# A two-block transformer step on one core: sums of squares as float32r products of a high and a low part

## The chip, the core and the metric

The kernel runs on one core of a Trainium2 chip. The metric is device microseconds of one execution, lower is better. Names: TensorE (PE; PEld is its weight load) does matrix products, VectorE (DVE) and ScalarE (ACT) elementwise work, GpSimd (POOL) little here, SyncE (SP) starts the DMAs.

## The reference, cut to what matters

One input of 256 rows of 1024 features (16 extra rows ahead in the first half) passes through two blocks. Everything is float32. The norms are what the change touches:

```
def rms_norm(x, g):                     # over all 1024 features, and over 64 of a head
    ms = mean(x * x, axis=-1)
    return x * rsqrt(ms + EPS) * g

# first block
h = h + 0.5 * swiglu(rms_norm(h), ...)                      # "f1", "d1"
# token mixer on rms_norm(h): two attentions of 8 heads
qa, ka = rms_norm(heads of h @ w_in)                        # each head of 64 by itself
qb, kb = rms_norm(heads of h @ w_in)
y = sigmoid(ga) * (attention(qa, ka, va) @ w) + sigmoid(gb) * (attention(qb, kb, vb) @ w)
h = h + y @ w_out
h = h + 0.5 * swiglu(rms_norm(h), ...)                      # "f2", "d2"
# second block: convolution and retention, cross attention, MLP, each on rms_norm(h)
```

So there are six norms over rows on the way (first FFN, token mixer, second FFN, second mixer, cross attention, MLP), a last one at the output that the change leaves alone, and head norms for 4 tiles of keys and 4 of queries of the first attention, 1 tile of keys and 4 of queries of the second: 13.

## The kernel before

Features lie on partitions (8 tiles of 128), rows of the sequence on the free axis (272 columns with the extra rows, else 256). Every large product is taken as three float32r products (`mm3`, lines 512 to 514): weight high x activation high, high x low, low x high. The weights come from memory in chunks of up to 2048 columns; `W.piece` cuts a piece of 1024 columns in two: ScalarE copies it rounded (`hi`, line 321), VectorE subtracts (`lo`, line 337). Three buffers each hold `raw`, `hi` and `lo`, so a new `hi` waits until TensorE has done with the chunk three back.

The order is written out by hand. `step` (a unit: 24 products or more on TensorE) first splits what the unit needs, issues the unit's products (`mm`), then a `hook` behind the split of the weights to come, and then the evacuations of the unit before, generators that give way to a weight piece at each `yield` and move to the next unit at `yield LATER`. What is issued stands in its engine's queue in that order.

The sums of squares over partitions are products with a constant matrix. `rms` (line 558), called as the hook of the first unit of a stage, multiplies `ones` (1/1024 everywhere) with `acc`, the squares summed over the 8 tiles, in float32, and takes the inverse root on ScalarE (lines 555, 556); every evacuation of the stage needs its result `r`. `head_norm` (line 761) squares x on ScalarE (`sqh`, line 765) and multiplies with `bd` (1/64 within a head), in float32 (line 767); the root follows a unit later. `key_like` and `query_like` call it in the unit after the projection. Between them on VectorE stand x (lines 803, 814), the writes of keys (line 828, six for a tile) and queries (lines 837, 851), and the values' multiplies (line 859), whose transposes (lines 865 to 867) stand on TensorE. The scores' first pass of the softmax is line 673, the transposes of its result lines 690 to 692.

PSUM has 8 banks in turn; during the two attentions three hold the results and five go round.

Of the kernel before, what the change touches and what calls it, by code (L numbers as in the profile page):

```python
# [11 lines left out]
F32R = mybir.dt.float32r  # L12
I32 = mybir.dt.int32
AF = mybir.ActivationFunctionType
# [3 lines left out]
P = 128  # L18
D = 1024
KD = D // P  # L20
SEQ = 256
NMETA = 16
T1 = SEQ + NMETA
# [341 lines left out]
LATER = object()  # L365
# [64 lines left out]
def _program(ctx, tc, I, out, probe=None):  # L430
    nc = tc.nc
    V, S, T = nc.vector, nc.scalar, nc.tensor
    probe = probe or (lambda name, ap: None)
    ctx.enter_context(tc.manual_schedule())
    base = ctx.enter_context(tc.tile_pool(name="base", bufs=1))
# [7 lines left out]
    def name(s):  # L443
        uid[0] += 1
        return f"{s}_{uid[0]}"
# [3 lines left out]
    def bank():  # L449

        turn[0] = (turn[0] + 1) % 8
        if spare[0] and turn[0] >= 5:
            return bank_o()
        return psum.tile([P, 512], F32, tag="ps", bufs=5, name=name("ps"))

    def bank_o():
        return psum_o.tile([P, 512], F32, tag="po", bufs=3, name=name("po"))

    def tmp(pool, tag, n=TP, bufs=2, dt=F32):
        t = pool.tile([P, -(-n // LINE) * LINE if pool is base else n], dt, tag=tag, bufs=bufs, name=name(tag))  # L460
        return t[:, :n]
# [3 lines left out]
    use, step, background = core.use, core.step, core.background  # L465
# [26 lines left out]
    def k0(n):  # L492
        o, w = _CST0[n]
        return c0[:, o : o + w]

    def kc(n):
        o, w = _CST[n]
        return cst[:, o : o + w]

    def c2(ap):  # L500
        return ap.rearrange("p (s c) -> p s c", c=P)
# [14 lines left out]
    def high(h_, src, gain=None):  # L516
        if gain is None:
            S.activation(h_, src, AF.Copy)
        else:
            S.activation(h_, src, AF.Copy, scale=gain)  # L520

    def low(l_, src, h_, gain=None):
        if gain is None:
            V.tensor_tensor(l_, src, h_.bitcast(F32), op=ALU.subtract)
        else:
            V.scalar_tensor_tensor(l_, src, gain, h_.bitcast(F32), op0=ALU.mult, op1=ALU.subtract)  # L526
# [25 lines left out]
    def rsqrt(dst, src):  # L552

        use(LN_EXP)
        S.activation(dst, src, AF.Ln, bias=k0("eps")[: dst.shape[0]])
        S.activation(dst, dst, AF.Exp, scale=-0.5)

    def rms(acc, n):

        ps = bank()  # L560
        T.matmul(ps[:, :n], k0("ones"), acc, start=True, stop=True)
        r = tmp(base, "r")
        rsqrt(r[:, :n], ps[:, :n])
        return r

    def xs(k, n=SEQ):
        return XH[:, k, :n], XL[:, k, :n]

    def next_acc():
        return tmp(base, "acc")  # L570
# [21 lines left out]
    def ffn(f, d, n, h, gain, acc_in, acc_out, bg, together):  # L592
        with tc.tile_pool(name="ffn" + f, bufs=2, reuse_waits="tile") as pool:
# [5 lines left out]
            def stats():  # L599
                r.append(rms(acc_in[:, :n], n))  # L600
# [127 lines left out]
    def mixer(acc_in, acc_out):  # L728
        with tc.tile_pool(name="mixer", bufs=1, reuse_waits="tile") as pool:
# [28 lines left out]
            def project(tag, ms, evac, n=SEQ, width=P, **kw):  # L758
                products(tag, ms, lambda k: xs(k, n), evac, late=1, out=lambda t: t[:width, :n], **kw)

            def head_norm(x, n):


                sq = tmp(pool, "sqh")[:, :n]
                S.activation(sq, x, AF.Square)
                ss = bank()
                T.matmul(ss[:, :n], kc("bd"), sq, start=True, stop=True)

                def root():
                    rc = tmp(pool, "rc")[:, :n]  # L770
                    rsqrt(rc, ss[:, :n])
                    return rc

                return root
# [26 lines left out]
            def key_like(ps, write):  # L801
                x = tmp(pool, "x", bufs=4)[:, :T1]
                V.tensor_tensor(x, ps[:, :T1], r[0][:, :T1], op=ALU.mult)
                yield
                root = head_norm(x, T1)
                yield LATER
                rc = root()
                yield
                for e in range(2):
                    write(e, slice(64 * e, 64 * e + 64), x, rc)  # L810

            def factor(dst, ps, turned):
                order = backwards if turned else lambda ap: ap
                V.tensor_tensor(dst, order(c2(ps[:, :SEQ])), order(c2(r[0][:, :SEQ])), op=ALU.mult)

            def query_like(ps, write, turned=False):
                x = tmp(pool, "x", bufs=4)[:, :SEQ]
                factor(c2(x), ps, turned)
                root = head_norm(x, SEQ)
                yield LATER  # L820
                rc = root()
                yield
                write(x, rc)
# [63 lines left out]

            use(LN_EXP)
            project("ka", (0, 1, 2), key, T1, hook=lambda: r.append(rms(acc_in[:, :T1], T1)))
            project("ka", (3,), key, T1)  # L890
            for m in range(4):
# [652 lines left out]
    acc = next_acc()  # L1544
# [6 lines left out]
    for k in range(KD):  # L1551
        squares(acc[:, :T1], hA[:, k, :T1], k, T1)()
        if k % 4 == 3:
            W.piece(2 * CH)
    W.split(2 * CH)
    background.append(lambda: None)
    background.append(lambda: None)
    background.append(lambda: nc.sync.dma_start(cst, I["cst"]))

    acc2 = next_acc()  # L1560
    with tc.tile_pool(name="early", bufs=1, side="right") as early:
# [8 lines left out]
    acc, acc2 = acc2, next_acc()  # L1570
# [3 lines left out]
    acc, acc2 = acc2, next_acc()  # L1574
# [11 lines left out]
    acc, acc2 = acc2, next_acc()  # L1586
    with tc.tile_pool(name="kvm", bufs=1, side="right", reuse_waits="tile") as kv:
# [5 lines left out]
        acc, acc2 = acc2, next_acc()  # L1593
        cross(acc, acc2, kx, vx, rm, held)
        probe("h5", hB)
    acc, acc2 = acc2, next_acc()
# [17 lines left out]
```

## Time and profile before

| | |
|---|---|
| median of three runs | 960.11 us (959.51 to 960.20) |
| the profiled execution | 959.74 us, its span 958.0 us |
| TensorE busy | 939.4 us, 98% |
| VectorE busy | 672.9 us, 70% |
| ScalarE busy | 534.7 us, 56% |
| HBM read | 166.79 MB, 175 GB/s over the span |

A busy share is taken over the whole span. Matmul records overlap, since they are pipelined: their distance from start to start tells what one costs in a stream. The profiled execution lies 0.37 us under the median of the three runs.

### The profile page before, as it was taken

To read this page: it belongs to the slowest core of one execution; us is meant where nothing else is said; L and a number is where in the kernel's file an instruction comes from. 1 tells how busy PE (TensorE), PEld (TensorE's weight loads), DVE (VectorE), ACT (ScalarE), POOL (GpSimd) and SP (SyncE) were. 2 spreads that over 40 slices of the span, in tenths; PEclk is the share of its full clock that TensorE was granted. 3 is DMA by queue.
4 is the path that set the end of the run, shared out by engine and by line. 5 is a ranking of instruction groups with operands and counts; after the bars stand their busy time and mean duration, and the time that the engine had idled before them with its cause. 6 is when DMAs were issued, how large, how long until landed. Compare 5 with 4: busy or idle time off the path is not lost.

```text
span 958.0 us, 18402 instructions
## 1 busy us (share of the span) xinstructions
PE 939.4 (98%) x7667; PEld 911.9 (95%) x7667; DVE 672.9 (70%) x1249; ACT 534.7 (56%) x927; POOL 9.9 (1%) x15
## 2 busy tenths in 40 slices
PE   7999999999999999999999999999999999999996
PEld 7999999998998999999999999889899999999996
DVE  5686556667885768677666657999977577775552
ACT  7545435456585656666554447646485466554441
POOL 0000000020000000000000000000000000000000
PEclk9999999999999999999999999999999999999998
DMA  8675526544432335565545665433544256555431
GB/s 309 192 259 181 180 94 222 175 175 160 171 126 96 133 114 217 221 220 184 210 152 180 214 214 235 168 140 134 195 162 171 88 177 221 199 200 218 176 133 44
DMA packets 31364, 169.06 MB, mean 176 GB/s; under 512 B 5144, under 2 KB 8864, under 8 KB 14640
## 3 DMA queue, kind: packets, MB, share of 16 engines
q1 hardware_dynamic: 30928, 167.34, 50.1%
q8 instruction: 60, 0.98, 0.4%
q10 hardware_dynamic: 288, 0.52, 0.1%
q14 instruction: 24, 0.20, 0.1%
q0 software_dynamic: 64, 0.01, 0.0%
HBM read 166.79 MB, written 1.07 MB: 175 GB/s over the span
## 4 chain that ended last, share of the span: by engine, by line
PE 72%; ACT 1%; DVE 1%; issue 0%; DVEq 0%
PE ps L512 14%; PE ps L513 14%; PE ps L514 14%; PE po L513 7%; PE po L514 7%; PE po L512 7%; PE ps L1015 1%; PE ps L1013 1%; PE ps L1014 1%; PE ps L661 1%; PE ps L1316 1%; PE po L705 0%; PE ps L1182 0%; PE po L1354 0%; PE po L720 0%; PE ps L1354 0%
## 5 line engine op out<-in xcount | busy, mean ns | idle before, releaser
L337 DVE TENSOR_TENSOR lo<-raw,hi 128x1024 fp32r<-128x1024 f32 (+2 forms) x334 | 373.7, 1131 | 46.2 <-ACT hi L321 44.2
L321 ACT ACTIVATE hi<-raw 128x1024 fp32r<-128x1024 f32 (+2 forms) x334 | 322.3, 981 | 127.4 <-issue 40.8
L512 PE MATMUL ps<-XH,hi 128*128 128x256 f32 (+2 forms) x976 | 280.2, 287 | 6.9 <-ACT hi L321 4.4
L514 PE MATMUL ps<-XH,lo 128*128 128x256 f32 (+2 forms) x976 | 274.7, 281 | 0.8 <-DVE lo L337 0.8
L513 PE MATMUL ps<-XL,hi 128*128 128x256 f32 (+2 forms) x976 | 274.9, 282 | 0.0
L512 PEld LDWEIGHTS ps<-XH,hi 128*128 128x128 f32 (+1 forms) x976 | 183.9, 188 | 10.5 <-ACT hi L321 4.4
L513 PEld LDWEIGHTS ps<-XL,hi 128*128 128x128 f32 (+1 forms) x976 | 184.3, 189 | 1.3 <-DVE XL L526 0.5
L514 PEld LDWEIGHTS ps<-XH,lo 128*128 128x128 f32 (+1 forms) x976 | 183.9, 188 | 1.4 <-DVE lo L337 1.0
L512 PE MATMUL po<-XH,hi 128*128 128x256 f32 (+1 forms) x456 | 128.9, 283 | 0.2 <-DVE br L1079 0.2
L514 PE MATMUL po<-XH,lo 128*128 128x256 f32 (+1 forms) x456 | 127.7, 280 | 0.6 <-DVE lo L337 0.6
L513 PE MATMUL po<-XL,hi 128*128 128x256 f32 (+1 forms) x456 | 127.5, 280 | 0.0
L514 PEld LDWEIGHTS po<-XH,lo 128*128 128x128 f32 x456 | 85.7, 188 | 0.8 <-DVE lo L337 0.8
L512 PEld LDWEIGHTS po<-XH,hi 128*128 128x128 f32 x456 | 85.7, 188 | 0.6 <-DVE br L1079 0.4
L513 PEld LDWEIGHTS po<-XL,hi 128*128 128x128 f32 x456 | 85.7, 188 | 0.1
L620 ACT ACTIVATE s<-gr 128x272 f32<-128x272 f32 (+1 forms) x44 | 18.7, 426 | 104.4 <-DVE gr L618 104.4
L512 PE MATMUL ps<-AHf,hi 128*128 128x272 f32 (+1 forms) x220 | 61.9, 281 | 0.0
L513 PE MATMUL ps<-ALf,hi 128*128 128x272 f32 (+1 forms) x220 | 61.9, 281 | 0.0
L514 PE MATMUL ps<-AHf,lo 128*128 128x272 f32 (+1 forms) x220 | 61.9, 281 | 0.0
L1053 DVE SCALAR_TENSOR_TENSOR cv<-U,par,cv 128x256 f32<-128x256 f32 x120 | 50.0, 474 | 0.2 <-ACT cv L1086 0.2
L514 PE MATMUL ps<-AHm,lo 128*128 128x256 f32 x160 | 44.2, 276 | 0.0
L512 PE MATMUL ps<-AHm,hi 128*128 128x256 f32 x160 | 44.2, 276 | 0.0
L513 PE MATMUL ps<-ALm,hi 128*128 128x256 f32 x160 | 44.2, 276 | 0.0
(384 smaller groups left out, 1769.2 us busy)
## 6 DMA issues: line engine op xcount, KB each, us to landing
raw<-in_ws_dram SPq DMA_DIRECT2D x128, 1024.0 KB, 4.8
raw<-in_ws_dram SPq DMA_DIRECT2D x32, 704.0 KB, 4.2
raw<-in_ws_dram SPq DMA_DIRECT2D x3, 512.0 KB, 5.3
dec<-in_dec_dram SPq DMA_DIRECT2D x1, 1536.0 KB, 6.6
BM<-drow SPq DMA_DIRECT2D x2, 512.0 KB, 5.5
memraw<-in_mt_dram SPq DMA_DIRECT2D x1, 1024.0 KB, 6.9
hA<-in_xt_dram SPq DMA_DIRECT2D x3, 273.0 KB, 5.4
raw<-in_ws_dram SPq DMA_DIRECT2D x3, 256.0 KB, 6.0
```

Source lines behind the costliest of these rows:

```text
L321: self.nc.scalar.activation(self.hi[c][:, a:b], self.raw[c][:, a:b], AF.Copy)
L337: self.nc.vector.tensor_tensor(self.lo[c][:, a:b], self.raw[c][:, a:b], self.hi[c][:, a:b].bitcast(F32), op=ALU.subtract)
L512: T.matmul(o, w[0], x[0], start=start, stop=False)
L513: T.matmul(o, w[0], x[1], start=False, stop=False)
L514: T.matmul(o, w[1], x[0], start=False, stop=stop)
L620: S.activation(s, gr, AF.Silu)
L661: T.matmul(ps[h][:, at : at + n], lhs, rhs, start=True, stop=True)
L1013: T.matmul(ps[i], xh[:, t], wh, start=k == 0, stop=False)
L1014: T.matmul(ps[i], xl[:, t], wh, start=False, stop=False)
L1015: T.matmul(ps[i], xh[:, t], wl, start=False, stop=k == KD - 1)
L1053: V.scalar_tensor_tensor(cv[:, m], U[:, m, j : j + SEQ], prm("cw", m * 31 + j), cv[:, m], op0=ALU.mult, op1=ALU.add)
L1316: T.matmul(ps[:, qt * SEQ : (qt + 1) * SEQ], qx[:, 2 * h + j, qt * P : (qt + 1) * P], kx[:, 2 * h + j], start=j == 0, stop=j == 1)
```

## The change

A sum over partitions now takes its operand in two float32r parts: `high` copies it rounded on ScalarE, `low` subtracts on VectorE, and `sum_over` issues two float32r products with a rounded copy of the constant matrix (`wr`, made once by `exact`). The 1/1024 and 1/64 are powers of two, so the rounded matrix is the same matrix. For the heads, the square takes a buffer under the tag "rc" (two buffers), which the roots use as well; the parts have the tags "sh" and "sl" (two buffers each). In `query_like` the parts are made where the sum was, and the sum is issued behind a further `yield LATER`, one unit later. In `key_like` the sum stays in its unit. Five entries more stand in the list of background work.

```
+    def two_parts(h_, l_, x):
+        high(h_, x)
+        low(l_, x, h_)
+        return h_, l_
+
+    def sum_over(o, w, parts):
+        for i, part in enumerate(parts):
+            T.matmul(o, w, part, start=i == 0, stop=i == 1)
+
     def rms(acc, n):
+        parts = two_parts(*(tmp(base, "sq", dt=F32R)[:, :n] for i in range(2)), acc)
         ps = bank()
-        T.matmul(ps[:, :n], k0("ones"), acc, start=True, stop=True)
+        sum_over(ps[:, :n], wr[:, 0], parts)
...
+    wr = base.tile([P, 2, P], F32R, name="wr")
+    def exact(i, w):
+        high(wr[:, i], w)
...
-            def head_norm(x, n):
-                sq = tmp(pool, "sqh")[:, :n]
+            def squared_parts(x, n):
+                sq = tmp(pool, "rc", T1)[:, :n]
                 S.activation(sq, x, AF.Square)
+                return two_parts(*(tmp(pool, "s" + c, T1, dt=F32R)[:, :n] for c in "hl"), sq)
+
+            def head_norm(parts, n):
                 ss = bank()
-                T.matmul(ss[:, :n], kc("bd"), sq, start=True, stop=True)
+                sum_over(ss[:, :n], wr[:, 1], parts)
                 def root():
-                    rc = tmp(pool, "rc")[:, :n]
+                    rc = tmp(pool, "rc", T1)[:, :n]
...
             def key_like(ps, write):
-                root = head_norm(x, T1)
+                root = head_norm(squared_parts(x, T1), T1)
                 yield LATER
...
             def query_like(ps, write, turned=False):
-                root = head_norm(x, SEQ)
+                parts = squared_parts(x, SEQ)
+                yield LATER
+                root = head_norm(parts, SEQ)
                 yield LATER
...
+    exact(0, k0("ones"))
...
+    background.extend([lambda: None] * 4)
+    background.append(lambda: exact(1, kc("bd")))
```

What stands where. First ScalarE at the start of the token mixer, from the norm over rows to the fourth key; `hi` are weight pieces, `r` the root of the norm, `sqh` (then `rc`) the squares of the keys. Before:

```order
L321 ACTIVATE hi_2440<-raw_2398 128x1024 x2
L321 ACTIVATE hi_2520<-raw_2444 128x1024
L555 ACTIVATE r_2528<-ps_2526,c_72 128x272
L556 ACTIVATE r_2528<-r_2528 128x272
L321 ACTIVATE hi_2520<-raw_2444 128x1024
L765 ACTIVATE sqh_2560<-x_2556 128x272
L765 ACTIVATE sqh_2566<-x_2564 128x272
L765 ACTIVATE sqh_2572<-x_2570 128x272
L321 ACTIVATE hi_2603<-raw_2524 128x1024
L765 ACTIVATE sqh_2609<-x_2601 128x272
```

The same place after:

```order
L321 ACTIVATE hi_2448<-raw_2406 128x1024 x2
L321 ACTIVATE hi_2528<-raw_2452 128x1024
L518 ACTIVATE sq_2534<-acc_171 128x272
L555 ACTIVATE r_2541<-ps_2538,c_72 128x272
L556 ACTIVATE r_2541<-r_2541 128x272
L321 ACTIVATE hi_2528<-raw_2452 128x1024
L779 ACTIVATE rc_2573<-x_2569 128x272
L518 ACTIVATE sh_2575<-rc_2573 128x272
L779 ACTIVATE rc_2584<-x_2582 128x272
L518 ACTIVATE sh_2586<-rc_2584 128x272
L779 ACTIVATE rc_2595<-x_2593 128x272
L518 ACTIVATE sh_2597<-rc_2595 128x272
```

The norm's copy (`sq<-acc`) stands behind the weight piece ahead of the root, and each key's copy (`sh`) behind its square. The other five norms have the copy at the same place.

VectorE there, from the norm to the fourth key. Before:

```order
L337 TENSOR_TENSOR lo_2441<-raw_2398,hi_2440 128x1024 x2
L803 TENSOR_TENSOR x_2556<-ps_2435,r_2528 128x272
L337 TENSOR_TENSOR lo_2521<-raw_2444,hi_2520 128x1024
L803 TENSOR_TENSOR x_2564<-ps_2436,r_2528 128x272
L803 TENSOR_TENSOR x_2570<-ps_2437,r_2528 128x272
L803 TENSOR_TENSOR x_2601<-ps_2531,r_2528 128x272
L337 TENSOR_TENSOR lo_2521<-raw_2444,hi_2520 128x1024
```

After:

```order
L337 TENSOR_TENSOR lo_2449<-raw_2406,hi_2448 128x1024 x2
L524 TENSOR_TENSOR sq_2535<-acc_171,sq_2534 128x272
L822 TENSOR_TENSOR x_2569<-ps_2443,r_2541 128x272
L337 TENSOR_TENSOR lo_2529<-raw_2452,hi_2528 128x1024
L524 TENSOR_TENSOR sl_2576<-rc_2573,sh_2575 128x272
L822 TENSOR_TENSOR x_2582<-ps_2444,r_2541 128x272
L524 TENSOR_TENSOR sl_2587<-rc_2584,sh_2586 128x272
L822 TENSOR_TENSOR x_2593<-ps_2445,r_2541 128x272
L524 TENSOR_TENSOR sl_2598<-rc_2595,sh_2597 128x272
L822 TENSOR_TENSOR x_2629<-ps_2544,r_2541 128x272
L337 TENSOR_TENSOR lo_2529<-raw_2452,hi_2528 128x1024
L524 TENSOR_TENSOR sl_2640<-rc_2637,sh_2639 128x272
```

Ahead of the first key stands the norm's subtraction (`sq<-acc,sq`), and between one key's multiply and the next the subtraction `sl`.

VectorE again, from the fourth query's multiply to that of the first value unit (`x` and `rep`). Before:

```order
L814 TENSOR_TENSOR x_2793<-po_2726,r_2528 128x256
L337 TENSOR_TENSOR lo_2761<-raw_2720,hi_2760 128x1024
L837 SCALAR_TENSOR_TENSOR qz<-x_2751,gq,rc_2799 64x256 x2
L778 TENSOR_TENSOR p_2831<-ps_2768,r_2528 8x272
L779 TENSOR_SCALAR p_2831<-p_2831,par 8x272
L780 SCALAR_TENSOR_TENSOR p_2832<-p_2831 8x272
L837 SCALAR_TENSOR_TENSOR qz<-x_2793,gq,rc_2839 64x256 x2
L859 TENSOR_TENSOR x_2869<-ps_2806,r_2528 128x256
L861 TENSOR_TENSOR rep_2871<-ps_2806,r_2528 128x128
```

After:

```order
L833 TENSOR_TENSOR x_2833<-po_2761,r_2541 128x256
L524 TENSOR_TENSOR sl_2838<-rc_2835,sh_2837 128x256
L337 TENSOR_TENSOR lo_2801<-raw_2757,hi_2800 128x1024
L858 SCALAR_TENSOR_TENSOR qz<-x_2742,gq,rc_2844 64x256 x2
L797 TENSOR_TENSOR p_2876<-po_2808,r_2541 8x272
L798 TENSOR_SCALAR p_2876<-p_2876,par 8x272
L799 SCALAR_TENSOR_TENSOR p_2877<-p_2876 8x272
L858 SCALAR_TENSOR_TENSOR qz<-x_2786,gq,rc_2887 64x256 x2
L880 TENSOR_TENSOR x_2917<-ps_2851,r_2541 128x256
L882 TENSOR_TENSOR rep_2919<-ps_2851,r_2541 128x128
```

The last query's pair of multiplies (`qz`) no longer stands ahead of the value unit's `x`, the third's stands behind the forget gate's work (`p`), and the subtraction of the fourth query stands ahead of all of them.

## Rows read from the trace of the kernel before

**Rows 1.** The page's table of engines: busy us (share of the span) xinstructions

```profile
PE 939.4 (98%) x7667; PEld 911.9 (95%) x7667; DVE 672.9 (70%) x1249; ACT 534.7 (56%) x927; POOL 9.9 (1%) x15
```

**Rows 2.** Timeline of TensorE at the second norm: start, us, engine, line, out<-in, xcount

```profile
217.22 0.29 PE L514 MATMUL ps<-XH,lo 128*128 128x272 f32 x1
217.35 0.62 PE L561 MATMUL ps<-acc,c 128*128 128x272 f32 x2
...
217.93 0.29 PE L513 MATMUL ps<-XL,hi 128*128 128x272 f32 x1
```

**Rows 3.** Timeline of TensorE at two query sums; in brackets idle time and its releaser

```profile
229.71 0.70 PE L767 MATMUL ps<-sqh,cst 128*128 128x256 f32 x2 [1.11 <-ACT sqh L765]
...
236.94 0.70 PE L767 MATMUL po<-sqh,cst 128*128 128x256 f32 x2 [0.46 <-ACT sqh L765]
```

**Rows 4.** Timeline of ScalarE and TensorE at the first norm

```profile
21.74 2.01 ACT L321 ACTIVATE hi<-raw 128x1024 fp32r<-128x1024 f32 x2
...
22.64 0.28 PE L513 MATMUL po<-XL,hi 128*128 128x272 f32 x1
```

**Rows 5.** Timeline of the first FFN: a high part's copy and a low part's subtraction

```profile
29.60 0.43 ACT L518 ACTIVATE AHf<-a 128x272 fp32r<-128x272 f32 x1
...
30.68 0.44 DVE L524 TENSOR_TENSOR ALf<-a,AHf 128x272 fp32r<-128x272 f32 x1
```

**Rows 6.** Timelines at the second, third and fifth norm

```profile
217.10 1.06 ACT L321 ACTIVATE hi<-raw 128x1024 fp32r<-128x1024 f32 x1 [2.43 <-PE ps L513]
...
400.23 1.06 ACT L321 ACTIVATE hi<-raw 128x1024 fp32r<-128x1024 f32 x1 [4.93 <-PE ps L513]
...
401.37 0.28 PE L513 MATMUL po<-XL,hi 128*128 128x256 f32 x1
...
719.88 2.06 ACT L321 ACTIVATE hi<-raw 128x1024 fp32r<-128x1024 f32 x2
...
720.50 2.35 DVE L337 TENSOR_TENSOR lo<-raw,hi 128x1024 fp32r<-128x1024 f32 x2
...
721.68 0.28 PE L513 MATMUL po<-XL,hi 128*128 128x256 f32 x1
```

**Rows 7.** Timelines of VectorE, ScalarE and TensorE at the keys

```profile
219.03 0.44 DVE L803 TENSOR_TENSOR x<-ps,r 128x272 f32<-128x272 f32 x1 [2.73 <-ACT r L556]
...
220.52 1.13 DVE L803 TENSOR_TENSOR x<-ps,r 128x272 f32<-128x272 f32 x3
...
219.86 0.41 ACT L765 ACTIVATE sqh<-x 128x272 f32<-128x272 f32 x1
...
222.61 0.28 PE L513 MATMUL ps<-XL,hi 128*128 128x256 f32 x1
```

**Rows 8.** Timeline of VectorE: the writes of three keys, and of a query

```profile
224.07 4.68 DVE L828 SCALAR_TENSOR_TENSOR kz<-x,par,rc 64x128 f32<-64x128 f32 x18 [1.28 <-issue]
...
233.88 0.98 DVE L837 SCALAR_TENSOR_TENSOR qz<-x,gq,rc 64x256 f32<-64x256 f32 x2 [1.22 <-issue]
```

**Rows 9.** Timelines of VectorE and TensorE at the first value unit

```profile
245.63 0.42 DVE L859 TENSOR_TENSOR x<-ps,r 128x256 f32<-128x256 f32 x1
...
246.82 0.27 PE L865 MATMUL ps<-cst,x 128*128 128x128 f32 x1
```

**Rows 10.** Engines by window: us, busy (x) of PE, PEld, DVE, ACT, POOL, PEclk, DMA, GB/s

```profile
245.00:255.00 10.00, 10.00 (x85) 10.00 (x84) 9.54 (x27) 4.27 (x7) 0.00 (x0) 1.00 0.32 107
```

**Rows 11.** Timelines: a first pass of the second softmax; transposes of the first, next unit

```profile
270.95 0.44 DVE L673 CUSTOM_DVE_ANT_0 p<-ps,cst 128x272 f32<-128x272 f32 x1
...
272.95 0.27 PE L690 MATMUL ps<-cst,p 128*128 128x128 f32 x1
...
273.20 0.37 PE L512 MATMUL ps<-XH,hi 128*128 128x272 f32 x1
```

**Rows 12.** Engines by window, at the end of the span

```profile
949.00:952.00 3.00, 0.97 (x4) 0.30 (x2) 0.77 (x3) 1.81 (x4) 0.00 (x0) 1.00 0.00 0
952.00:955.00 3.00, 0.00 (x0) 0.00 (x0) 2.45 (x4) 0.00 (x0) 0.00 (x0) 0.56 0.49 182
```

## The prediction

> **What bounds the kernel now.** I read the page's table of engines first, then TensorE's own waits, then the timelines of all engines round each changed sum. TensorE is busy for 98% of the span [rows 1], and its timeline is all but gapless from the first weights to the last product. It runs its matmuls in the order of the program: a product whose operand is late holds every one behind it [rows 3]. So a changed sum is worth what it does to TensorE's start of the next unit, and nothing else.
>
> **The float32 sum itself.** In [rows 2] the last projection product starts at 217.22, the sum (two recorded passes) at 217.35, and the second product behind it at 217.93. Matmuls of this size start 0.13 apart, so of those 0.71 us the two ordinary products take 0.26 and a float32 sum 0.45. Two float32r products should take 0.26 again. Gain 0.2 each; with 6 norms over rows and 13 over heads that is 19 x 0.2 = 3.8 us. The queries' sums also waited: 1.11 us at 229.71 and 0.46 at 236.94 [rows 3]; issuing them a unit later removes that, another 1.6 us. All this is gain if the two parts lie ready when TensorE gets there.
>
> **What a sum now needs first.** The high part is a copy on ScalarE: 0.43 us; the low part a subtraction on VectorE: 0.44 us [rows 5] (0.42 at 256 columns, as other instructions of that width take [rows 9]). With a handoff of 0.04 us each that is 0.95 us more between the squares and the second product. Both stand in queues that do nothing out of order, behind what the unit has put there.
>
> **The six norms over rows.** rms() is called behind a unit's products and behind the split of the next weights, so the copy stands behind ScalarE's weight piece. First norm, at 22 us: the pieces of 21.74 end at 23.75, the copy of the constant matrix ahead of them adds some 0.2 (an estimate, half of a copy of 272 columns), but an instruction may start 0.1 before its forerunner's recorded end: copy 23.85 to 24.28, subtraction to 24.76, second product 24.80, then the unit's second matmul at 25.05 instead of 22.64 [rows 4]: 2.4 us later. Before, the sum did not wait here, since the squares were summed long before. Second norm: ScalarE's piece begins only at 217.10, because its buffer comes free as the unit ends [rows 6]; copy to 218.50, subtraction to 218.98, second matmul 219.26 instead of 217.93: 1.3 us. Third: the piece ends at 401.29, the parts at 401.61 and 402.07, the matmul of 401.37 moves to 402.34: 1.0 us. The pattern of the second stands once more (782 us, 1.3), that of the third once more (582 us, 1.0). In the fifth the subtraction stands behind two weight pieces that end at 722.85 [rows 6]: 722.78 to 723.20, the matmul of 721.68 moves to 723.47: 1.8 us. What follows each waits for r, which moves by as much, so no second wait is added. Sum, with the gain of 0.2 inside each: 2.4 + 1.3 + 1.0 + 1.0 + 1.8 + 1.3 = **8.8 us**. From below, were each copy first in its queue, 0.95 less 0.2 each, 4.5 us for six; from above, the 8.8 with 0.5 for each further piece that slips in front, 11.
>
> **The keys.** Times are now the rows' own, with the shift of the norms ahead taken off. Before, the multiplies x of keys 2 to 4 stood back to back on VectorE (three in 1.13 us) and the squares followed on ScalarE [rows 7]. Now each key's multiply, square, copy and subtraction follow one another, since the subtraction stands ahead of the next key's multiply. First key: square 219.86 to 220.27, copy to 220.73, subtraction to 221.21. A further key takes 0.44 + 0.41 + 0.43 + 0.44 and the handoffs, less the overlaps: 1.74 us. The third's subtraction ends at 224.69. TensorE has only these sums next in its queue and starts the first query unit's second matmul at 224.96 instead of 222.61 [rows 7]: 2.35 us late. It gets most of that back where the first query's sum (1.8 us with its wait) leaves its old place: 0.3 us late at 230.7. Here the idea works.
>
> **VectorE's backlog.** But VectorE has lost time for good. Each serial round costs it 1.4 us (a subtraction, and a wait of 1.0 for square and copy) where nothing stands between. Lag behind its own rows: 3.4 after three keys; 2.7 at the first query, since the wait of 1.28 at 224.07 takes some up [rows 8]; 3.8 at the second; 3.3 at the third (the multiply pair of 0.98 moves behind, and the wait of 1.22 at 233.88 goes [rows 8]); 4.5 at the fourth; **5.6 us** at the multiply of the first value unit, 251.2 instead of 245.63 [rows 9]. That multiply's transposes stand in TensorE's queue: they start at 251.66 instead of 246.82, 4.8 us late. From here VectorE is 95% busy [rows 10] and cannot catch up. The pair moved behind adds 1.0 (6.6). The next key's subtraction (0.35) is about balanced by a wait that goes, and three more query rounds come before the second softmax: +4.1, less some 0.8 that VectorE itself waited there and one multiply of 0.4 moved behind: 9.4 us. There TensorE is held by PSUM: with five banks in turn, the second group of transposes at 272.95 takes the bank of the second pair's first scores, which VectorE reads at 270.95 for 0.44 [rows 11]. Plus 9.4 that ends at 280.8, and the other head's bank, for the unit at 273.20 [rows 11], at 281.4. TensorE is **8.2 us** late, with the sums' gain inside. It had slack of 1.5 us at that bank before, so a small lag would have cost nothing. Bounds: 4.8, if VectorE's waits shrink after the values; 10.5, if TensorE follows its whole lag and a later bank adds 1.
>
> **Free.** Two copies of the constant matrices; five empty steps in the list of background work, which shift the bias matmuls and tables by one or two units in the first FFN, where TensorE waits for none of them; DMAs of that list pass one weight load on SP's queue, far ahead of its use.
>
> **Sum.** 8.8 + 8.2 = 17.0 us on the profiled execution of 959.74 (span 958.0): 976.7. The median of the three runs is 0.37 above that, so **977 us** (1.8%).
>
> **Rivals.** (a) *The parts are ready and the cheaper products show.* Faster by 3.8 + 1.6 = 5.4: 954.7 us. It decides where copy and subtraction get in before TensorE arrives. For it: queries at 230.7 above. Against: in every norm a piece of ScalarE's that ends after the old sum's start (four of them in [rows 4, 6]), and the serial keys. 5%. A half-way case, stalls of 5.4 us in all that eat up the gain, 3%.
> (b) *VectorE catches up.* Were its backlog gone by the values, the mixer would cost only the 0.3 us found at 230.7: 959.7 + 8.8 + 0.3, with the 0.37: 969 us. For it: VectorE waits for TensorE in most other stages. Against: 95% in [rows 10]. 14%.
> (c) *The clock falls.* The granted clock was full until 952 us and 0.56 of full in the three after it, so at the lower level (1.2 GHz) for most of them, when TensorE had done 0.97 us of work in the three before [rows 12]. The new stalls leave TensorE nearly idle for about 2.7 us (first norm), 4 us (keys) and 3.4 us (first value). If it falls at the first norm or behind the mixer, matmuls stand twice as far apart; over 4 us (an estimate) that is 2 us each time. In keys and values VectorE's lag hides it. One or two falls: 979 to 982. 22%. The Trainium skill, "TensorE: Matmul & The Clock Gate", section "Why this matters for your kernels", warns that an idle gap between bursts of matmuls brings the lower clock back. By that rule the change pays a second time for each long stall and the time is 979 or more; the end of this trace agrees that the clock can fall within three microseconds of dense work.
> (d) *It doesn't do what it says:* each new product costs what the old sum did. 19 x (0.90 - 0.26) = 12 us more, 989. Against: other products of that type start 0.13 apart [rows 2]. 2%.
>
> **How the numbers follow.** Forecast 54%, (a) with the half-way case 8%, (b) 14%, (c) 22%, (d) 2%. A measurement of this kernel can tell about 0.2% from no change. Faster 0.05, same 0.03, slower 0.92. The low end takes in (b), the high end (c) and the upper bounds of norms and mixer: 969 to 984.
>
> **What would show it.** Right: TensorE waits at all six norms' sums for the copy or the subtraction, 1 to 2.5 us each; waits in the three keys' sums; a wait of some 3 us at the first value's transposes, released by VectorE; TensorE 8 us late by the second pair's transposes. Wrong: sums that stand in the stream with no idle time before them (a); VectorE idle between the values and the second softmax (b); a granted clock below 1 before 940 us (c); a sum's two products 0.4 or more apart with both parts ready (d). The weakest step is the backlog, because it adds up eight rounds worked by hand.

## The result, and the profile after

The changed kernel takes 982.22 us (median of four runs, 981.8 to 984.4) against 960.15 for the kernel before, measured beside it: a ratio of 1.0231, 95% interval 1.0218 to 1.0243. The forecast was 977.0 with a range of 969 to 984. The direction was right and the time lies within the range, 5.2 us above the point. The profiled execution took 982.4 us, its span is 980.6, that is 22.6 more than before.

The page's table of engines, to be held against [rows 1]:

```profile
PE 948.4 (97%) x7667; PEld 917.6 (94%) x7667; DVE 680.2 (69%) x1268; ACT 543.4 (55%) x948; POOL 9.9 (1%) x15
```

TensorE has as many matmuls as before and each of the new sums is cheaper, yet it is *busy* for 9.0 us longer. Waits alone give a part of it, since a product beside a gap is recorded longer (0.39 us for a sum's product, 0.28 in a stream). The rest is the first sign that some of its matmuls ran slower. TensorE's waits in the trace after (engine, what it was to start, what released it: us in total, times, longest):

```profile
PE po L566 <- ACT sq L518: 3.5, 2, 2.5
PE ps L566 <- ACT sq L518: 3.4, 4, 1.0
PE ps L886 <- DVE x L880: 3.3, 1, 3.3
PE po L566 <- ACT sh L518: 1.8, 2, 0.9
PE ps L706 <- DVE mn L689: 1.7, 1, 1.7
...
PE po L566 <- DVE sq L524: 0.6, 1, 0.6
```

L566 is `sum_over`. The two rows with `sq` are the six norms over rows (the low part of the fifth stands in the last row), the row with `sh` is the keys, L886 the first value's transposes, L706 the transposes behind the second softmax. None of these is in the trace before.

To split the 22.6 us, I took the same product in both traces, a stage further each time, and noted how much later it starts (for instance 298.17 after for 282.80 before). What each stage adds:

| stage | forecast, us | measured, us |
|---|---|---|
| start, until 20 us | 0 | 0.7 |
| norms over rows, first to sixth | 2.4, 1.3, 1.0, 1.0, 1.8, 1.3 = 8.8 | 2.9, 1.4, 1.1, 1.1, 2.0, 1.4 = 9.9 |
| mixer, from the norm to the wait behind the second softmax | 8.2 | 8.3 |
| the 10 us behind that wait | 0 | 2.1 |
| rest of the mixer | 0 | 0.1 |
| the 7 us behind the fourth norm | 0 | 1.6 |
| sum | 17.0 | 22.7 |

The first row is not the change's. In the other runs, two of which change nothing so early, TensorE reaches the first norm between 0.3 us sooner and 1.1 us later than before.

The second norm in the timeline of ScalarE, VectorE and TensorE (start, us, engine, line, out<-in, count, in brackets idle time and its releaser):

```profile
220.71 1.06 ACT L321 ACTIVATE hi<-raw 128x1024 fp32r<-128x1024 f32 x1 [2.42 <-PE ps L513]
221.67 0.41 ACT L518 ACTIVATE sq<-acc 128x272 fp32r<-128x272 f32 x1
222.12 0.44 DVE L524 TENSOR_TENSOR sq<-acc,sq 128x272 fp32r<-128x272 f32 x1 [2.20 <-ACT sq L518]
222.14 0.87 PE L566 MATMUL ps<-sq,wr 128*128 128x272 f32 x2 [1.02 <-ACT sq L518]
...
222.84 0.29 PE L512 MATMUL ps<-XH,hi 128*128 128x272 f32 x1
```

ScalarE stood idle for 2.42 us ahead of the weight piece, whose buffer TensorE still held; the copy stood behind that piece. This is the order that [rows 6] and the listing of the change had promised.

The keys on VectorE:

```profile
225.76 0.44 DVE L524 TENSOR_TENSOR sl<-rc,sh 128x272 fp32r<-128x272 f32 x1 [0.16 <-ACT sh L518]
226.12 0.43 DVE L822 TENSOR_TENSOR x<-ps,r 128x272 f32<-128x272 f32 x1
227.51 0.44 DVE L524 TENSOR_TENSOR sl<-rc,sh 128x272 fp32r<-128x272 f32 x1 [0.96 <-ACT sh L518]
227.87 0.43 DVE L822 TENSOR_TENSOR x<-ps,r 128x272 f32<-128x272 f32 x1
229.26 0.44 DVE L524 TENSOR_TENSOR sl<-rc,sh 128x272 fp32r<-128x272 f32 x1 [0.96 <-ACT sh L518]
```

Before, three multiplies stood back to back [rows 7]. Now each waits for the subtraction ahead of it, and that for square and copy, 0.96 us in the second and third round: 1.75 us for a key. The lag reaches the first value and the second softmax. VectorE first:

```profile
256.32 0.42 DVE L880 TENSOR_TENSOR x<-ps,r 128x256 f32<-128x256 f32 x1
...
285.42 0.43 DVE L689 CUSTOM_DVE_ANT_0 p<-ps,cst 128x272 f32<-128x272 f32 x1
```

and TensorE:

```profile
256.80 0.48 PE L886 MATMUL ps<-cst,x 128*128 128x128 f32 x1 [3.27 <-DVE x L880]
...
285.92 0.33 PE L706 MATMUL ps<-cst,p 128*128 128x128 f32 x1 [1.67 <-DVE mn L689]
```

The multiply is 10.69 us later than in [rows 9], the softmax pass 14.47 later than in [rows 11]. Less the 5.0 of start and norms that is a lag of 5.7 and 9.4; the forecast was 5.6 and 9.4.

TensorE by window (us, busy and matmuls, granted clock, DMA share, GB/s), at the four places where the clock fell:

```profile
226.00:230.00 4.00, 2.04 (x6) 0.94 0.01 2
230.00:233.00 3.00, 3.00 (x15) 0.52 0.32 44
252.00:257.00 5.00, 1.73 (x14) 0.98 0.00 0
257.00:260.00 3.00, 3.00 (x15) 0.50 0.00 0
284.00:288.00 4.00, 2.29 (x16) 0.94 0.50 213
288.00:291.00 3.00, 3.00 (x15) 0.51 0.00 0
598.00:602.00 4.00, 2.98 (x18) 0.94 0.48 201
602.00:606.00 4.00, 4.00 (x25) 0.63 0.00 0
```

A granted clock of 0.5 is the lower level, 1.2 GHz. In each pair the first window has TensorE partly idle, the second has it fully busy with products that start twice as far apart:

```profile
599.21 0.84 PE L566 MATMUL ps<-sq,wr 128*128 128x256 f32 x2 [0.71 <-ACT sq L518]
...
601.53 0.58 PE L512 MATMUL po<-XH,hi 128*128 128x256 f32 x1 [0.24 <-DVE br L1100]
...
602.12 0.41 PE L514 MATMUL po<-XH,lo 128*128 128x256 f32 x1
602.33 0.41 PE L512 MATMUL ps<-XH,hi 128*128 128x256 f32 x1
```

The first two lines are TensorE's only waits at the fourth norm, and the second of them stands in the trace before as well; products of this size start 0.11 apart in the trace before, here 0.21.

### The profile page after: what moved, and what is told of

Read it like the earlier page. It is cut to its first block, busy times and chain, and to the rows that moved or that the text cites. A ratio compares the mean times of both kernels' runs of the same rounds, so it can differ in the third digit from the quotient of the medians.

```text
span 980.6 us, 18449 instructions
## 1 busy us (share of the span) xinstructions
PE 948.4 (97%) x7667; PEld 917.6 (94%) x7667; DVE 680.2 (69%) x1268; ACT 543.4 (55%) x948; POOL 9.9 (1%) x15
## 4 chain that ended last, share of the span: by engine, by line
PE 85%; DVE 7%; ACT 5%; issue 1%; DMA 1%; SPq 1%; DVEq 0%; ACTq 0%
PE ps L512 16%; PE ps L514 16%; PE ps L513 16%; PE po L514 9%; PE po L512 9%; PE po L513 9%; DVE lo L337 2%; ACT hi L321 1%; PE ps L1036 1%; PE ps L1034 1%; PE ps L1035 1%; DMA raw<-in_ws_dram 1%; PE ps L677 1%; DVE acc L535 1%; DVE kz L849 1%
## 5 line engine op out<-in xcount | busy, mean ns | idle before, releaser
L512 PE MATMUL ps<-XH,hi 128*128 128x256 f32 (+1 forms) x976 | 280.6, 288 | 6.6 <-ACT hi L321 4.1
L514 PE MATMUL ps<-XH,lo 128*128 128x256 f32 (+1 forms) x976 | 276.7, 284 | 1.1 <-DVE lo L337 1.1
L513 PE MATMUL ps<-XL,hi 128*128 128x256 f32 (+1 forms) x976 | 276.6, 283 | 0.0
L512 PEld LDWEIGHTS ps<-XH,hi 128*128 128x128 f32 x976 | 186.9, 192 | 9.8 <-ACT hi L321 4.1
L514 PEld LDWEIGHTS ps<-XH,lo 128*128 128x128 f32 x976 | 186.6, 191 | 1.7 <-DVE lo L337 1.6
L513 PEld LDWEIGHTS ps<-XL,hi 128*128 128x128 f32 x976 | 187.1, 192 | 0.7 <-DVE XL L526 0.5
L512 PE MATMUL po<-XH,hi 128*128 128x256 f32 (+2 forms) x456 | 129.2, 283 | 0.2 <-DVE br L1100 0.2
L514 PE MATMUL po<-XH,lo 128*128 128x256 f32 (+2 forms) x456 | 128.5, 282 | 0.6 <-DVE lo L337 0.6
L513 PE MATMUL po<-XL,hi 128*128 128x256 f32 (+2 forms) x456 | 128.5, 282 | 0.0
L512 PEld LDWEIGHTS po<-XH,hi 128*128 128x128 f32 (+1 forms) x456 | 85.9, 188 | 1.2 <-ACT s L636 0.5
```

Of the source, the lines that this page charges most:

```text
L512: T.matmul(o, w[0], x[0], start=start, stop=False)
L513: T.matmul(o, w[0], x[1], start=False, stop=False)
L514: T.matmul(o, w[1], x[0], start=False, stop=stop)
```

## The experiments

They ran on three chips, on which the kernel before took 960.7 to 961.2 us in the median; each time below stands beside the ratio to the kernel before on the same chip. How late TensorE is at a stage is read in each run's trace as above. For the mixer, from its norm to the product at 282.80 of before, and for the lower clock, all of them together:

| run | the mixer adds, us | the granted clock fell behind |
|---|---|---|
| the changed kernel | 10.4 | keys, first value, second softmax, fourth norm |
| norms_only | 0.0 | fifth norm |
| heads_only | 10.5 | keys, first value |
| norms_early | 10.7 | keys, first value, second softmax |
| no_low | 3.0 | first norm, first value, fourth norm |
| low_on_pool | 3.2 | keys, fourth norm |
| no_round | 2.8 | fourth norm |
| filled | 9.5 | nothing |
| queries_late | 0.3 | nothing |
| all_early | 2.8 | keys |

**One part at a time.** norms_only keeps `rms` of the changed kernel and takes the heads back; heads_only the reverse:

```
# norms_only
-                root = head_norm(squared_parts(x, T1), T1)
+                root = head_norm(x, T1)              # keys and queries: square and float32 sum
# heads_only
-        parts = two_parts(..., acc)
-        sum_over(ps[:, :n], wr[:, 0], parts)
+        T.matmul(ps[:, :n], k0("ones"), acc, start=True, stop=True)
```

> The six norms over rows as in the changed kernel, the heads' sums as before (float32, queries' sums in their old unit). In the two traces TensorE's delay grows by about 2.9, 1.7, 1.4, 0.9, 2.3 and 1.4 us at the six norms, 10.7 in all (the prediction had 8.8), and by another 1.4 us in the stretch at the lower granted clock behind the fourth. If norms and heads add up and the clock falls at the fourth norm here too: 960.2 + 12.1 = 972.3 us. If the clock falls there only because the mixer's stalls went before: 970.9. If part of the 10.7 belongs to the heads: 969.0, as the prediction had it.

> The heads' sums as in the changed kernel, the norms over rows as before (float32). By the two traces the token mixer costs 10.1 us (8.1 up to the second softmax, which the prediction had at 8.2, and about 2 behind it, 1.5 of them at the lower clock): 970.3 us. If the clock behind the second softmax fell only because the norm ahead had stalled too: 968.5. If VectorE catches up without the norm's delay ahead of it: 961. The stretch at the lower clock at about 600 us of the changed kernel should be gone.

norms_only: 974.58 us (972.4 to 978.1), ratio 1.0148 [1.0123, 1.0173]. heads_only: 971.62, ratio 1.0110 [1.0095, 1.0126]. The two excesses, 1.48% and 1.10%, give 2.58% together, against 2.31 for the whole change: they add up within their intervals, so either part loses by itself. The norms add 12.0 us in the trace of norms_only, some 1.5 of that at the lower clock behind the *fifth* norm, which adds 3.8 here and 2.0 in the changed kernel (the rest is a subtraction that comes 0.3 later):

```profile
589.00:593.00 4.00, 3.24 (x21) 1.00 0.31 131
728.00:732.00 4.00, 2.08 (x14) 0.93 0.20 78
732.00:736.00 4.00, 4.00 (x25) 0.64 0.75 262
```

Behind the fourth (the first row) the clock stayed up here, though TensorE's two waits there are the same to the hundredth, 0.71 and 0.24 us. By this run alone the fall there could have needed the mixer's stalls; but no_round, below, has it with no fall in the mixer. Which stall is followed by one differs from run to run. In heads_only no clock fell behind the second softmax, as its second expectation had it, and yet the mixer cost the same. In place of the fall stands a wait of 0.82 us, and the stretches in the keys and behind the first value lasted about twice as long. The second one was not wholly hidden: VectorE itself waits 0.69 us for a product of TensorE at 268.98, and its pass of the second softmax is 10.5 us late, not 9.4.

**Where the parts stand in the queue.** norms_early makes the norms' parts as soon as the squares are summed; the products stay:

```
     def step(self, key, mm, ..., pre=None):
+        if pre:
+            pre()                     # two_parts(..., acc), ahead of the weight pieces
         W.split(end)
         mm()
```

> The changed kernel with one thing moved: the norms' two parts are made as soon as the squares are summed, ahead of the weight pieces, instead of behind them. The products stay. If the place in ScalarE's and VectorE's queues is the cause of the norms' stalls, the six waits go and each sum is 0.2 us cheaper than before: 982.2 - 10.7 - 1.4 (the lower clock at the fourth norm) - 1.2 = 969 us. If the round of copy and subtraction itself is the cause, whatever stands ahead of it, 4.5 us of stalls stay: 974. If the weight pieces that are now pushed back by 0.8 us become late for TensorE, waits for hi or lo appear behind the norms, and the time is above 974.

974.05 us, ratio 1.0135 [1.0119, 1.0151], nearer to the 974 than to the 969. But the reason is not the one given for 974; it is the third, weight pieces that come late. No wait for a norm's part is left in the trace; the second norm on ScalarE and TensorE:

```profile
213.99 0.43 ACT L520 ACTIVATE sq<-acc 128x272 fp32r<-128x272 f32 x1
...
219.40 1.06 ACT L321 ACTIVATE hi<-raw 128x1024 fp32r<-128x1024 f32 x1 [2.12 <-PE ps L515]
...
219.52 0.29 PE L516 MATMUL ps<-XH,lo 128*128 128x272 f32 x1
219.65 0.41 PE L568 MATMUL ps<-sq,wr 128*128 128x272 f32 x2
219.90 0.29 PE L514 MATMUL ps<-XH,hi 128*128 128x272 f32 x1
```

The copy is done 5 us ahead of its use, and the whole sum takes 0.25 us from start to start. The place in the queue was the norms' cause: all stages but the start and the mixer add 2.4 us here, in the changed kernel 11.6 with the fall behind the fourth norm. The 2.4 are not at the sums, which gain 0.2 us each: a wait of 1.19 us for a low weight piece stands at 30.86, and some 1.6 us come in the second FFN and the second mixer. The mixer still adds 10.7.

**VectorE standing still.** Three ways to free VectorE of the heads' rounds: leave the subtraction out, put it on GpSimd, or issue the same instructions in rows:

```
# no_low
+                return sh, sh                       # the high part twice
# low_on_pool
+            on.tensor_tensor(l_, x, h_.bitcast(F32), op=ALU.subtract)    # on = nc.gpsimd
# no_round: three keys
+                parts = [square_high(x, T1, i == 2) for i, x in enumerate(xs_)]
+                parts = [head_low(p) for p in parts]
+                roots = [head_norm(p, T1) for p in parts]
# no_round: every other head
+                parts = square_high(x, SEQ)
                 yield LATER
+                root = head_norm(head_low(parts), SEQ)
```

> The changed kernel with the heads' subtraction on VectorE left out: the high part is multiplied twice, so TensorE's work is the same, but the heads' sums are no longer those of the reference. Square and copy on ScalarE stay. If VectorE's rounds (subtract, wait for square and copy) make the mixer's 10.1 us, that and its stretches at the lower clock go, the cheaper products show, and the time is 982.2 - 10.1 - 1.6 = 970.5 us, no wait at the first value's transposes. If ScalarE's longer chain (square, then copy) makes it, whatever VectorE does, 10 us stay: 982.

> The changed kernel with the heads' 13 subtractions on GpSimd, which is idle in the mixer (1% of the span), instead of VectorE. All sums are right. If VectorE's place in the chain is the cause, VectorE no longer stands still for each key, and the mixer's cost falls to the keys' own delay (some 2 to 3 us, longer if GpSimd takes longer than 0.44 us for one): 972 to 975 us. If the longer chain to TensorE is the cause, 982 or more.

> The changed kernel with the same instructions in another order for the heads: the first three keys' multiplies, squares, copies and subtractions in rows instead of key by key, and every other subtraction one unit later, just ahead of its sum, so that VectorE never stands still for ScalarE. If the standing still makes the lag (1.0 of the 1.4 us of each round), about 13 x 0.44 = 5.7 us of VectorE work stay in the way, of which the sums' 2.6 and the queries' waits take some back: the mixer costs some 3 to 5 us instead of 10.1, in all 975 to 977. If the plain amount of VectorE work decides, not the order: 982. If nothing is left of the lag: 971.

no_low 977.01 us, ratio 1.0171 [1.0156, 1.0186]; low_on_pool 974.75, 1.0138 [1.0121, 1.0155]; no_round 974.60, 1.0142 [1.0127, 1.0157]. In all three the mixer's cost falls from 10.4 to about 3. low_on_pool came out in the first range of its expectation, no_round just below the first of its own. no_round decides it, since it has all the subtractions on VectorE still. Its keys:

```profile
224.78 0.78 DVE L831 TENSOR_TENSOR x<-ps,r 128x272 f32<-128x272 f32 x2
225.48 0.43 DVE L524 TENSOR_TENSOR sq<-sqh,sh 128x272 fp32r<-128x272 f32 x1
226.18 0.44 DVE L524 TENSOR_TENSOR sq<-sqh,sh 128x272 fp32r<-128x272 f32 x1 [0.26 <-ACT sh L518]
226.96 0.44 DVE L524 TENSOR_TENSOR p<-rc,p 128x272 fp32r<-128x272 f32 x1 [0.34 <-ACT p L518]
```

Waits of 0.26 and 0.34 instead of 0.96 twice. It was the standing still, not the work: 7.5 of the 10.4 us are a matter of order, the lower clock behind the second softmax, which went with its stall, among them. no_round also gives the parts other buffers and issues the other keys' sums a unit later; the buffers are not it, since low_on_pool keeps them and falls as far; what the later sums give by themselves no run shows. The 2.8 left are above the 0.3 of the queries' move alone (below); I did not take them apart further.

no_low missed its 970.5 by 6.5 us: 3.0 of the mixer's cost stayed, and the 1.6 taken off besides did not show. Contrary to its expectation the first value's transposes still wait 3.0 us for VectorE, since TensorE, with the queries' sums moved, gets there 1.7 us ahead. The clock fell behind its first norm as well:

```profile
24.00:28.00 4.00, 3.71 (x15) 0.58 0.67 240
```

That norm adds 3.7 us with it, 0.7 more than in the changed kernel, though its wait is shorter, 1.70 us for 2.53.

**Is it idling that lowers the clock?** filled gives TensorE products that nobody reads in its stalls:

```
+    def fill_in(o, n, times):
+        for _ in range(times):
+            T.matmul(o[:, :n], wr[:, 0], XH[:, 0, :n], start=True, stop=True)
```

> The changed kernel with products that nobody reads in TensorE's stalls: 4 to 18 ahead of each norm's sum and 3 or 6 repeats of its first product, the same in the first keys, 24 ahead of the first value's transposes, 26 small ones in the second softmax's wait. They start at once and end before the awaited operand comes, so the stalls keep their length, but TensorE is not idle in them. If idling is what lowers the clock, the stretches at the lower clock (keys, first value, second softmax, fourth norm, 5.5 us in all) go. Those behind the second softmax and the fourth norm are worth 2.9 us of time: 979.3. Those in the keys and at the first value are hidden by VectorE's lag and give nothing; were they not hidden, 976.7. If the clock falls for another reason: 982.2.

980.68 us, ratio 1.0206 [1.0191, 1.0221]. The granted clock is full everywhere the changed kernel's was not:

```profile
226.00:230.00 4.00, 3.79 (x28) 1.00 0.01 2
230.00:233.00 3.00, 3.00 (x28) 1.00 0.34 49
257.00:260.00 3.00, 2.73 (x23) 1.00 0.00 0
288.00:291.00 3.00, 3.00 (x26) 1.00 0.00 0
602.00:606.00 4.00, 4.00 (x38) 1.00 0.00 0
```

Same stalls, same change, and no fall: with TensorE kept busy in its stalls the clock stayed up, so idle time is what it followed. The ratio is 0.25% lower than the changed kernel's (2.4 us; the intervals just touch); 2.9 were expected, and the fillers of the second softmax held the unit behind it 0.7 us longer than its bank. Up to that wait the mixer adds 9.0 us here, those 0.7 included, with the clock up throughout, and 8.3 in the changed kernel, with two falls inside it. VectorE's pass of the second softmax, in filled

```profile
285.88 0.44 DVE L696 CUSTOM_DVE_ANT_0 p<-ps,cst 128x272 f32<-128x272 f32 x1
```

is 9.4 us late in both, once the start and the norms ahead, 5.5 us here, are taken off. So the two falls in keys and values cost nothing in the changed kernel: TensorE only reached VectorE's next late result with less time to wait.

**The queries' move alone**, in float32 on the kernel before:

```
                 factor(c2(x), ps, turned)
+                sq = squared(x, SEQ)
+                yield LATER
                 root = head_norm(sq, SEQ)
```

> Only the move: the kernel before with the queries' sums one unit later, in float32, no parts anywhere. The sums' two waits of 1.11 and 0.46 us go, and nothing is added on VectorE or ScalarE: 960.2 - 1.6 = 958.6 us. If the waits are only passed on to a later wait on VectorE: 960.2.

961.46 us, ratio 1.0012 [0.9999, 1.0025]: nothing gained. TensorE does get ahead, by 2.0 us up to the last query, and gives it back at the values:

```profile
246.62 0.33 PE L870 MATMUL ps<-cst,x 128*128 128x128 f32 x1 [0.64 <-DVE x L864]
250.87 0.30 PE L870 MATMUL po<-cst,x 128*128 128x128 f32 x1 [0.73 <-DVE x L864]
257.97 0.33 PE L870 MATMUL ps<-cst,x 128*128 128x128 f32 x1 [0.31 <-DVE x L864]
```

These waits are new. VectorE sets the pace at that place as soon as TensorE gets ahead, without any of the change's subtractions.

**The five empty entries**, on the kernel before:

```
     background.append(lambda: nc.sync.dma_start(cst, I["cst"]))
+    background.extend([lambda: None] * 5)
```

> The kernel before with one edit: five empty entries behind the DMA of the constant matrices in the list of background work, as the change has them, and no part of any sum changed. By the prediction they cost nothing: 960.2 us. By the traces of the heads alone and of the early norms, where TensorE waits 0.84 and 1.19 us for a low weight piece at about 30 us, a wait that the bias products, now moved behind, had covered: 961.2.

961.76 us, ratio 1.0008 [0.9998, 1.0017]. That doesn't tell 0 from 1 us. In its trace there is no wait at 30 us and no loss behind the start, but TensorE had started 1.0 us later there, so the weight piece had that much more time; in heads_only, which started 0.2 late, the wait is there with 0.84. Open, and at most about 1 us.

**Versions meant to keep the gain.** early_norms_only is norms_early with the heads in float32 and without the entries; all_early joins norms_early, no_round and GpSimd's subtractions, also without the entries; all_early_pool moves nine small additions of the forget gates to GpSimd as well:

```
# all_early
+    exact(1, kc("bd"))                                       # just ahead of the mixer
+                nc.gpsimd.tensor_tensor(sl, sq, sh.bitcast(F32), op=ALU.subtract)
# all_early_pool, besides
+                    gp.tensor_tensor(b[:, 256:], a[:, 256:], a[:, 256 - s : 256 + T1 - s], op=ALU.add)
```

> The norms alone in two parts, made as soon as the squares are summed, the heads' sums as before in float32, and none of the five extra entries in the background list. If the cheaper products are worth what their places show (0.2 us each) and the parts are ready: 960.2 - 1.2 = 959.0 us, 0.9988 of before. If the fifth norm, whose squares are summed just before its sum, still waits 0.4 us, and weight pieces pushed back by 0.8 us cost a wait or two: 960 to 961, no difference that can be measured. If queue position was not the cause of the norms' stalls: 969.

> Both parts of the change with what the runs so far recommend: the norms' parts made early, the heads' instructions in the order of the run with rows of keys, their subtractions on GpSimd, one unit ahead of the sum, and the rounded matrix for the heads made just ahead of the mixer, without the five entries. If standing still and queue position were all that the change cost, the mixer costs nothing and the 19 cheaper products show where TensorE sets the pace (norms 1.2 us, heads up to 2.6): 957 to 960. If the mixer still loses 2.5 us, as it did with GpSimd or with rows of keys alone, because its keys wait: 961.5. If GpSimd's 0.75 us for a subtraction is too slow ahead of the sums: above 963.

> The run with everything early, and the nine additions of the forget gates' running sum (8 partitions, 0.43 us each on VectorE) moved to GpSimd too. If VectorE's load between the queries and the second softmax is what keeps the kernel from gaining more, 3.9 us less of it there is worth up to as much as the values' waits for x are long, 1.5 us: 955.5 to 958. If GpSimd's nine additions (some 0.8 us each) make the keys' last rows late for the first scores, a wait appears there and the time is above the run with everything early.

early_norms_only: 961.58 us, ratio 1.0006 [0.9997, 1.0015]. Four norms gain 0.2 us each, just what [rows 2] had promised; the gain goes again in waits, 0.49 for a low weight piece at 23.31, 0.27 for another at 577.38, and 0.42 for the keys' squares at 222.62. The last is not the norms': five_empty and queries_late have 0.4 there too, and I don't know its cause. all_early: 964.10, ratio 1.0041 [1.0025, 1.0058]; its keys wait for GpSimd, which takes 0.76 us for the subtraction, and for the second key 1.44, where VectorE takes 0.44:

```profile
223.00 0.39 PE L568 MATMUL po<-sq,wr 128*128 128x272 f32 x1 [0.46 <-POOL sq L797]
...
224.81 0.39 PE L568 MATMUL po<-sq,wr 128*128 128x272 f32 x1 [1.13 <-POOL sq L797]
...
225.54 0.59 PE L568 MATMUL po<-p,wr 128*128 128x272 f32 x1 [0.21 <-POOL p L797]
```

The clock falls behind them once more. all_early_pool: 965.12, ratio 1.0044 [1.0032, 1.0056]. No version beats the kernel before.

## Why the prediction was right, and where it was short

**The bound.** TensorE's order was the right thing to follow. A sum with its parts ready takes 0.25 us where the float32 sum took 0.45, as [rows 2] said.

**The norms.** Right in kind, 8.8 forecast and 9.9 measured. All six wait, for the copy or the subtraction; the third and fourth wait 0.7 us, less than the 1 us given as a sign, but add what was forecast. The first is the largest miss, 2.9 for 2.4: ScalarE's pieces of [rows 4] began at 23.04 instead of 21.74, 1.3 us later, TensorE's last product only 0.7, since the start of the run set the two engines apart; the estimate had the two move together. norms_early shows that the queue was the cause.

**Keys and VectorE's backlog.** The step called the weakest held. The keys' sums wait 0.88 twice, not three times: the first key's high part came just in time, and its low part held the second product by some 0.3 us. At 230.7 TensorE is 1.9 us late and not 0.3, because the clock is down there; filled has 0.5. The lag is 5.7 us at the first value (5.6), where TensorE is 5.0 late (4.8), and 9.4 at the second softmax (9.4, though the terms as written add to 9.5), TensorE 8.3 late there (8.2). no_round shows that the waiting inside a round, 1.0 of 1.4 us, was the expensive part, as the forecast had it.

**The queries' gain.** That the move is worth 1.6 us, as the first part of the working says, is wrong: queries_late measured none. In the forecast's sum it did no harm, because VectorE's lag, not the sums' gain, set TensorE's time there. In rival (a) it was a part of the 5.4 us, so that rival was priced too well.

**Free.** The five entries were said to cost nothing. In heads_only and norms_early, where no norm stalls ahead of it, TensorE waits 0.84 and 1.19 us for a weight piece at about 30 us; that the bias products, which the entries move, had covered its arrival is argued and not shown, since five_empty has no such wait. In the changed kernel itself there is none, behind the first norm's stall.

**The clock: the term that was mis-sized.** The forecast had it at zero, and rival (c) at 22%, with one or two falls of 2 us behind the first norm or the mixer, and hidden ones in keys and values. What happened is (c): four falls, two of them hidden as said, one behind the mixer and one behind the fourth norm, where the price was 1.6 us each. (Two falls at its own price make 981, where it wrote 982.) That the time lies in the range is owed to the high end, which took in (c); the point, 977, left it out. Sum: 17.0 + 3.2 for the clock + 1.1 for the norms + 0.7 for the start + 0.5 for two small waits behind the second softmax makes 22.5 of the 22.6. The mark for it, a granted clock below 1 before 940 us, stood in the prediction; the chance was too small. The forecast asked which single stall was long enough. It named the first norm, which the clock then survived, and the mixer, but not the fourth norm:

```profile
22.00:26.00 4.00, 1.38 (x10) 1.00 0.62 236
26.00:30.00 4.00, 4.00 (x33) 1.00 0.90 308
```

At that norm TensorE waits 2.53 us in one piece and the clock stays up; behind the fourth, with waits of 0.71 and 0.24 us, it fell. The rule that the prediction cited, of the Trainium skill, "TensorE: Matmul & The Clock Gate", section "Why this matters for your kernels", says that idle gaps between bursts bring the lower clock back. The four pairs of windows and filled agree with it; the first norm shows that a gap need not, since at the same place a wait of 1.70 us was followed by a fall in no_low and one of 2.53 by none here. So the length of a single stall did not tell which one would be followed by a fall, and what does stays open. The end of the trace before, too, is less quick than the prediction read it: the dense stream ends at 949.0 us, two more products stand at 950.26, and the clock is full until 952.

## What to carry to other kernels

A cheaper operation is worth its difference only if its operands lie ready where the bounding engine meets it; so price first where the new preparation stands in the in-order queues of the engines that make it, and behind what. Where one engine waits for another inside every unit, issue the steps in rows (all multiplies, then all squares, then all subtractions): issued in that order the mixer's change cost 3 us here instead of 10. And give every new stall of TensorE a second price: behind it the products may run at half the clock for some 3 us, which costs another 1.6 us unless some later wait swallows it.

## What the runs showed of the hardware

I had not expected the granted clock to fall behind stalls as short as these, with TensorE busy for 2.0 to 3.0 us of the 4 us windows ahead, nor that the same waits at the same norm would be followed by a fall in one run and not in another. One kernel's executions differ as well: two of norms_only took 972.4 and 972.9 us with a mean granted clock of 0.996, the other two 976.3 and 978.1 with 0.992 and 0.993. Where the clock fell in those two is not on record. Products without use in the stalls kept the clock at its upper level until the dense work ended. GpSimd's subtraction of 128x272 took 0.76 us beside VectorE's 0.44, and in each of the three runs with it one of the first keys took about 1.4.
